# Layer 1's up-projection as seven products of halves, from the third pair of units on

## The chip, the core and the metric

The kernel runs on one core of a Trainium2 chip. The metric is the device time of one execution in microseconds, the median of the runs of one kernel. Five engines of the core work side by side and are ordered by semaphores: TensorE (PE in the profile; PEld are its weight loads), VectorE (DVE), ScalarE (ACT), GpSimd (POOL), and SyncE (SP), on whose queue the loads are issued.

## The reference

Two layers of a backbone work on 512 latent and 256 context tokens of 1024 channels. A layer ends with a gated feed-forward part:

```python
def conv_ffn(xn, w_up, conv_w, w_down):
    u = dwconv(xn @ w_up, conv_w)          # width 3 over positions
    a, gt = jnp.split(u, 2, axis=-1)       # 2 x 2816 columns
    return (a * jax.nn.silu(gt)) @ w_down
```

All is float32. Layer 0 runs it for 768 tokens (latent and context), layer 1, the last one, for the 512 latent tokens only, since the context is no longer needed.

## The kernel before

Activations lie with channels on the 128 partitions and tokens along the free dimension. A float32 product is made of three matmuls of a rounded type (fp32r): each operand is split into a high part, a copy made by ScalarE, and a low part, the difference, made by DVE (`split`, lines 224 and 225). Then high x high, high x low and low x high are summed in PSUM (`mm3`, lines 264 to 266).

The feed-forward part (`ffn`) runs over the 22 blocks of 128 columns of each half of `w_up`, in pairs of two blocks. A pair has two units: g (the gate half) and a (the other half), 256 columns of weights each. Two pairs are a group of four blocks. In program order a group is g, the down-projection of the group before (`down`, held back until here), a, g, a, and then the next group's g. After each unit the convolution follows: one ScalarE step (line 1825) and two DVE steps (lines 1826 and 1828) a block; a g block then gets Silu (line 1834), an a block is multiplied with its g block on POOL (line 1843) and split for the down-projection (lines 1844 and 1845). The down-projection adds its PSUM result to the residual on DVE (line 1872). The last group's down-projection is `gemm_tail`.

A unit is computed in one of two ways:

- `gemm_fm`: for each of the two blocks a load of 128x1024 weights, a split, and 8 x 3 matmuls for each segment of tokens (512 latent, and 256 context in layer 0). The convolution reads PSUM directly.
- `gemm7` (lines 308 to 368): Strassen's method in Winograd's form on a unit seen as two by two halves (channels 0 to 511 and 512 to 1023; its two blocks) times two by two halves of the tokens. POOL makes four sums of halves of the weights (`half`, line 321); four weight tiles are split, w0, w23 and w1 of 128x1024 with the low part on DVE and w4 of 128x512 with the low part on POOL; seven products of 12 matmuls over half of the tokens (`prod`, line 334) use four PSUM tiles, of which three accumulate a second product; two ScalarE copies and five DVE sums (lines 353 to 365) bring the results to the SBUF tiles `c`, which the convolution reads.

The tokens' side of the seven products is made once by `norm_sums` (line 622): sums of halves of the tokens' parts `xh` and `xl` on DVE (line 633 and the two lines in `less`), split into the tiles `T`; the last one, `last_sum`, overwrites a quarter of `xh` and `xl` once the plain units are done. `norm_sums` is called with lowered priority beside the a unit of the second pair, and `x7` is set after it. In the kernel before this happens only where all 768 tokens are worked on (`nt == NT`), that is in layer 0: there pairs three to eleven (18 units) run `gemm7`, in layer 1 all units run `gemm_fm`, and the first g unit `gemm_first`.

Buffers: raw weights have 4 tiles of 128x1024 (tag `wraw`), the split weights 3 high and 3 low tiles (tags `wh`, `wl`), `s23` two and `s4` one; the pool `q6` has 11 tiles, shared by `R` and `T`, the split activations of the down-projection and the tail's weights. The order of each engine's instructions is set ahead by a planner (Tile), from the order of the program, priorities and its own estimates; on the chip each engine runs its list in order.

Of the kernel before, what the change touches and what calls it, by code (L numbers as in the profile page):

```python
# [10 lines left out]
F32R = mybir.dt.float32r  # L11
# [9 lines left out]
NT = SEQ + CTX  # L21
# [84 lines left out]
class Kernel:  # L106
# [515 lines left out]
    def norm_sums(self):  # L622


        nc, N = self.nc, self.N
        nm, n = N["nm"], N["nt"] // 2
        xh, xl = N["x"]
        q = lambda v, k, t: v[:, 4 * k:4 * k + 4, n * t:n * t + n]
        R = [self.q6(f"{nm}R{i}").rearrange("p (k t) -> p k t", k=4) for i in range(2)]
        T = {}  # L630

        def op(o, a, b, op):
            nc.vector.tensor_tensor(out=o, in0=a, in1=b, op=op)

        def diff(i, j, k):

            for o, v in zip(R, (xh, xl)):
                op(o, q(v, *j).bitcast(F32), q(v, *k).bitcast(F32), ALU.subtract)
            op(R[0], R[0], R[1], ALU.add)

        def less(o, j, a):
            op(o, q(xh, *j).bitcast(F32), a, ALU.subtract)
            op(o, o, q(xl, *j).bitcast(F32), ALU.add)

        def split(i, v):
            T[i] = [self.q6(f"{nm}T{p}{i}", F32R).rearrange("p (k t) -> p k t", k=4) for p in "hl"]
            self.split(*T[i], v)
        diff(1, (0, 1), (0, 0))
        split(1, R[0])
        less(R[1], (1, 1), R[0])  # L650
        split(3, R[1])
        less(R[0], (1, 0), R[1])
        split(4, R[0])
        diff(2, (1, 1), (0, 1))
        T[2] = q(xh, 0, 1), q(xl, 0, 1)

        def last():
            self.split(*T[2], R[0])
        return (xh, xl, T), last
# [1147 lines left out]
    def ffn(self, l, xs, nt):  # L1807
        nc = self.nc
        nm = f"f{l}"
        segb = [(0, SEQ)] + ([(SEQ, NT)] if nt == NT else [])  # L1810
        U, U2 = self.I["w_up"][l], self.I["w_down"][l]
        FG = 4
        down = None
        for f0 in range(0, NFF, FG):
            fn = min(FG, NFF - f0)
            gh, gl = [], []
            for p0 in range(0, fn, 2):
                keep = {}

                def conv(ch, res, tag):  # L1820
                    w = [self.V("fv", 132 * l + 44 * k + ch) for k in range(3)]
                    a = self.st(f"{nm}{tag}")
                    for ps, (s, e) in res:
                        n = e - s
                        nc.scalar.activation(a[:, s:e], ps, AF.Copy, scale=w[1])
                        nc.vector.scalar_tensor_tensor(out=a[:, s + 1:e], in0=ps[:, 0:n - 1], scalar=w[0],
                                                       in1=a[:, s + 1:e], op0=ALU.mult, op1=ALU.add)
                        nc.vector.scalar_tensor_tensor(out=a[:, s:e - 1], in0=ps[:, 1:n], scalar=w[2],  # L1828
                                                       in1=a[:, s:e - 1], op0=ALU.mult, op1=ALU.add)
                    return a  # L1830

                def done_g(b, ps):
                    a = conv(NFF + f0 + p0 + b, ps, f"g{f0}{p0}{b}")
                    nc.scalar.activation(a[:, :nt], a[:, :nt], AF.Silu)  # L1834
                    keep[b] = a

                def done_a(b, ps):
                    a = conv(f0 + p0 + b, ps, f"a{f0}{p0}{b}")
                    if b == 0:
                        gh.extend(self.pairs(f"{nm}gh{f0}{p0}", 1, F32R))  # L1840
                        gl.extend(self.pairs(f"{nm}gl{f0}{p0}", 1, F32R))
                    h = gh[-1][:, b, :nt]
                    nc.gpsimd.tensor_tensor(out=a[:, :nt], in0=a[:, :nt], in1=keep[b][:, :nt], op=ALU.mult)  # L1843
                    nc.scalar.copy(h, a[:, :nt])  # L1844
                    nc.vector.tensor_tensor(out=gl[-1][:, b, :nt], in0=a[:, :nt], in1=h.bitcast(F32), op=ALU.subtract)  # L1845

                if f0 + p0 == 0:
                    self.gemm_first(KD, xs, done_g, f"{nm}g{f0}{p0}")
                    x7 = None
                elif x7:  # L1850
                    self.gemm7(U, D_FF + 128 * (f0 + p0), x7, nt, done_g, f"{nm}g{f0}{p0}")
                else:
                    self.gemm_fm(U, D_FF + 128 * (f0 + p0), 256, KD, xs, done_g, f"{nm}g{f0}{p0}")
                if down and f0 + FG < NFF:
                    self.gemm_fm(*down)
                    down = None
                if f0 + p0 == 2 and nt == NT:
                    with self.high(-3000):
                        sums, last_sum = self.norm_sums()
                if x7:  # L1860
                    self.gemm7(U, 128 * (f0 + p0), x7, nt, done_a, f"{nm}a{f0}{p0}")
                else:
                    self.gemm_fm(U, 128 * (f0 + p0), 256, KD, xs, done_a, f"{nm}a{f0}{p0}")
                    if f0 + p0 == 2 and nt == NT:
                        x7 = sums
                        last_sum()
            segs = [((a, b), Blocks(gh, a, b), Blocks(gl, a, b)) for a, b in segb]

            def done_d(j, res):
                hv = self.hview(j)  # L1870
                for ps, (a, b) in res:
                    nc.vector.scalar_tensor_tensor(out=hv[:, a:b], in0=ps,
                                                   scalar=self.ada[l][:, 40 + j, (a >= SEQ):(a >= SEQ) + 1], in1=hv[:, a:b],
                                                   op0=ALU.mult, op1=ALU.add)
            if down:
                self.gemm_fm(*down)
            down = (U2[128 * f0:128 * (f0 + fn), :], 0, D, fn, segs, done_d, f"{nm}d{f0}")
        last = l == DEPTH - 1
        if not last:
            self.norm_begin(l + 1, 0, NT)  # L1880

        def done_t(j, seg, ps):
            done_d(j, [(ps, seg)])
            if not last:
                self.norm_sq(j, *seg, nc.vector if j % 2 else nc.gpsimd)
                if j == 5 and seg[0]:
                    rbs[seg[0] - 256, seg[0]] = self.norm_rs(seg[0] - 256, seg[0])
                if j == KD - 1 and seg[1] == nt:
                    rbs[seg] = self.norm_rs(*seg)
            elif j % 4 == 3:  # L1890
                self.store(j // 4, *seg)
        rbs = {}
        self.gemm_tail(down[0], segs, done_t, f"{nm}t",
                       None if last else (self.I["w_in"][l + 1], C_K, KD, f"c{l + 1}0k"))
        for seg, rb in rbs.items():
            self.norm_fin(*seg, rb)
        return None if last else self.N["xs"]
# [157 lines left out]
```

## Time and profile before

| | us |
|---|---|
| median of 3 runs | 2658.55 (2657.56 to 2661.77) |
| the profiled execution's own time | 2659.69 |
| its span | 2657.9 |
| layer 0's feed-forward part, first seven-product unit to tail | 1078 to 1543 |
| layer 1's feed-forward part, first unit to end | 2274 to 2658 |
| TensorE busy over the span | 2586.3 (97%) |

A page of the profile gives busy times of each engine; windows give them by stretch; a timeline gives single instructions with start and duration, and behind it, in brackets, how long the engine was idle before it and what released it. Matmuls overlap, so the duration of one (0.28 to 0.40 us) is longer than the distance from one start to the next; TensorE's pace is read from starts. Names such as f1a42p read: f, layer 1, a unit, group starting at block 4, pair 2 of it, p for PSUM (c and u for SBUF tiles, w0h and w0l for the high and low part of a weight tile, r for a raw weight tile).

### The profile page before, as it was taken

How to read it: one execution, taken by the hardware profiler on the slowest of the kernel's cores; microseconds unless marked ns; L12 is line 12 of the kernel's file. 1: busy time of each engine (PE TensorE's matmuls, PEld its weight loads, DVE VectorE, ACT ScalarE, POOL GpSimd, SP SyncE). 2: the span in 40 equal slices, each digit the busy share in tenths (PEclk: the TensorE clock that was granted, in tenths of full speed). 3: DMA queues.
4: the chain of work that ended last, by engine and by line, in shares of the span. 5: the costliest groups of instructions: out<-in, count | busy, mean ns of one | idle time of the engine just before them, and what ended most of it. 6: DMA issues, size and time to landing. Idle time of an engine off the chain costs nothing.

```text
span 2657.9 us, 44659 instructions
## 1 busy us (share of the span) xinstructions
PE 2586.3 (97%) x17185; PEld 2235.7 (84%) x17185; DVE 1689.9 (64%) x3599; ACT 1042.6 (39%) x2305; POOL 420.8 (16%) x348
## 2 busy tenths in 40 slices
PE   7999999999999999999999999999999999999999
PEld 5887988788888898899999988888877888888887
DVE  5766566756533648676787777856676646655555
ACT  4433446332422225343343454344633333433332
POOL 1000000000110421264245220000000103100000
PEclk9999999999999999999999999999999999999999
DMA  8354333556747423422212343522367674333332
GB/s 278 100 174 136 98 98 94 145 148 181 217 131 257 145 76 107 131 68 76 80 56 72 96 134 106 158 69 74 113 189 220 193 261 150 88 94 94 95 103 76
DMA packets 485222, 344.19 MB, mean 129 GB/s; under 512 B 48167, under 2 KB 450321, under 8 KB 484241
## 3 DMA queue, kind: packets, MB, share of 16 engines
q1 hardware_dynamic: 484721, 338.19, 42.7%
q8 instruction: 135, 2.21, 0.3%
q10 hardware_dynamic: 288, 3.15, 0.3%
q14 instruction: 78, 0.64, 0.1%
HBM read 285.23 MB, written 56.03 MB: 128 GB/s over the span
## 4 chain that ended last, share of the span: by engine, by line
PE 80%; DVE 8%; DMA 6%; issue 2%; ACT 1%; SPq 1%; POOL 1%; DVEq 0%; ACTq 0%; POOLq 0%
PE mg04p L265 2%; PE mg04p L266 2%; PE mg04p L264 2%; PE adp L541 1%; PE y0p L264 1%; PE y0p L265 1%; PE y0p L266 1%; PE mg14p L264 1%; PE mg14p L266 1%; PE mg14p L265 1%; PE y1p L264 1%; PE y1p L265 1%; PE y1p L266 1%; DMA ad<-ada_w 1%; PE y0op L265 1%
## 5 line engine op out<-in xcount | busy, mean ns | idle before, releaser
L1843 POOL TENSOR_TENSOR f1a<-f1a,f1g 128x512 f32<-128x512 f32 x22 | 28.5, 1295 | 312.1 <-DVE f1a L1828 292.6
L1843 POOL TENSOR_TENSOR f0a<-f0a,f0g 128x768 f32<-128x768 f32 x22 | 52.5, 2389 | 95.6 <-DVE f0a L1828 95.6
L541 PE MATMUL adp<-ad,s 128*32 128x256 f32 x640 | 54.4, 394 | 0.1
L1765 POOL TENSOR_TENSOR y0a<-y0a,y0g 128x768 f32<-128x768 f32 x16 | 33.2, 2078 | 118.1 <-DVE y0g L1762 115.8
L1120 POOL TENSOR_TENSOR m0qz<-m0qz,m0e 64x512 f32<-64x512 f32 x12 | 16.6, 1383 | 166.5 <-DVE b0a3P L1338 69.4
L544 ACT COPY adr<-adp 128x256 f32<-128x256 f32 x40 | 14.8, 371 | 49.4 <-PE adp L541 48.1
L541 PEld LDWEIGHTS adp<-ad,s 128*32 128x32 f32 x640 | 18.5, 110 | 18.5 <-issue 6.9
L1845 DVE TENSOR_TENSOR f0gl<-f0a,f0gh 128x768 fp32r<-128x768 f32 x22 | 28.3, 1287 | 8.9 <-ACT f0gh L1844 8.9
L1765 POOL TENSOR_TENSOR y1a<-y1a,y1g 128x512 f32<-128x512 f32 x16 | 24.2, 1514 | 60.6 <-DVE y1g L1762 60.6
L1844 ACT CAST f0gh<-f0a 128x768 fp32r<-128x768 f32 x22 | 18.4, 838 | 34.9 <-POOL f0a L1843 34.9
L1026 ACT ACTIVATE mg0t<-mg04p 128x512 f32<-128x512 f32 (+1 forms) x40 | 19.4, 486 | 26.2 <-PE mg04p L266 21.7
L1762 DVE SCALAR_TENSOR_TENSOR y0g<-y0g,y0p 128x512 f32<-128x512 f32 (+1 forms) x32 | 17.3, 548 | 15.4 <-PE y0p L266 14.0
L1120 POOL TENSOR_TENSOR m1qz<-m1qz,m1e 64x512 f32<-64x512 f32 x8 | 10.6, 1331 | 102.8 <-DMA m1qz<-aq 32.6
L1109 DVE SCALAR_TENSOR_TENSOR m0mb<-m0mb,g0a,cst 128x128 f32<-128x128 f32 x48 | 16.3, 398 | 16.4 <-DMA m0mb<-g0rd 15.5
L1834 ACT ACTIVATE f1g<-f1g 128x512 f32<-128x512 f32 x22 | 13.9, 630 | 32.5 <-DVE f1g L1828 32.5
L1834 ACT ACTIVATE f0g<-f0g 128x768 f32<-128x768 f32 x22 | 18.5, 846 | 20.5 <-DVE f0g L1828 20.5
L1786 DVE SCALAR_TENSOR_TENSOR hr<-y0op,y0gh,hr 128x512 f32<-128x512 f32 (+1 forms) x16 | 9.9, 616 | 25.5 <-PE y0op L266 25.5
L1182 POOL TENSOR_TENSOR rt<-rc,rw 128x256 f32<-128x256 f32 x4 | 4.2, 1042 | 119.7 <-DVE c00kq L1385 58.5
L1845 DVE TENSOR_TENSOR f1gl<-f1a,f1gh 128x512 fp32r<-128x512 f32 x22 | 15.1, 685 | 10.9 <-ACT f1gh L1844 10.7
L1742 DVE TENSOR_TENSOR y0l<-y0ld,y0h 128x768 fp32r<-128x768 f32 x12 | 12.8, 1090 | 11.6 <-ACT y0h L1741 11.6
L1844 ACT CAST f1gh<-f1a 128x512 fp32r<-128x512 f32 x22 | 13.5, 616 | 16.6 <-POOL f1a L1843 16.6
L1111 ACT ACTIVATE m0mb<-m0mb 128x512 f32<-128x512 f32 x12 | 7.6, 631 | 30.8 <-DVE m0mb L1109 25.3
(4525 smaller groups left out, 10177.4 us busy)
## 6 DMA issues: line engine op xcount, KB each, us to landing
ad<-ada_w SPq DMA_DIRECT2D x96, 512.0 KB, 4.1
mg04r<-w_in SPq DMA_DIRECT2D x20, 512.0 KB, 5.1
mg14r<-w_in SPq DMA_DIRECT2D x20, 512.0 KB, 5.9
y0g<-mg SPq DMA_DIRECT2D x24, 384.0 KB, 4.1
mg<-mg0t SPq DMA_DIRECT2D x24, 256.0 KB, 2.7
y0r<-w_branch SPq DMA_DIRECT2D x12, 512.0 KB, 3.5
mg<-mg1t SPq DMA_DIRECT2D x24, 256.0 KB, 4.2
y1r<-w_branch SPq DMA_DIRECT2D x12, 512.0 KB, 3.8
```

The source lines that it names most:

```text
L264: nc.tensor.matmul(o, hv[:, k, :], xh[:, k, :], start=(k == 0), stop=False)
L265: nc.tensor.matmul(o, hv[:, k, :], xl[:, k, :], start=False, stop=False)
L266: nc.tensor.matmul(o, lv[:, k, :], xh[:, k, :], start=False, stop=(k == nk - 1))
L541: nc.tensor.matmul(ps[32 * j:32 * j + 32, 0:256], self.s32[:, 2 * k:2 * k + 32], raw[:, j, :], start=(q == 0), stop=(q == 1), tile_positio ...
L1026: nc.scalar.activation(s, o, AF.Tanh, scale=0.5)
L1120: nc.gpsimd.tensor_tensor(out=qd[r, d], in0=qd[r, d], in1=e2[r], op=ALU.mult)
L1762: nc.vector.scalar_tensor_tensor(out=(a if i == BR[0] else gt)[:, s:e], in0=gt[:, s:e], scalar=1.0, in1=ps, op0=ALU.add, op1=ALU.mult)
L1765: nc.gpsimd.tensor_tensor(out=a[:, :nt], in0=a[:, :nt], in1=gt[:, :nt], op=ALU.add)
L1834: nc.scalar.activation(a[:, :nt], a[:, :nt], AF.Silu)
L1843: nc.gpsimd.tensor_tensor(out=a[:, :nt], in0=a[:, :nt], in1=keep[b][:, :nt], op=ALU.mult)
L1844: nc.scalar.copy(h, a[:, :nt])
L1845: nc.vector.tensor_tensor(out=gl[-1][:, b, :nt], in0=a[:, :nt], in1=h.bitcast(F32), op=ALU.subtract)
```

## The change

`norm_sums` and `x7` no longer ask for all 768 tokens, so layer 1 too runs its pairs three to eleven (18 units) through `gemm7`, with halves of 256 tokens. The tiles `R` and `T` are cut to the size that the tokens need (4 x 256 columns of 1536). Nothing else differs; the order of units and down-projections in the program is the one that layer 0 has.

```diff
@@ norm_sums
-        R = [self.q6(f"{nm}R{i}").rearrange("p (k t) -> p k t", k=4) for i in range(2)]
+        R = [self.q6(f"{nm}R{i}")[:, :4 * n].rearrange("p (k t) -> p k t", k=4) for i in range(2)]
...
-            T[i] = [self.q6(f"{nm}T{p}{i}", F32R).rearrange("p (k t) -> p k t", k=4) for p in "hl"]
+            T[i] = [self.q6(f"{nm}T{p}{i}", F32R)[:, :4 * n].rearrange("p (k t) -> p k t", k=4) for p in "hl"]
@@ ffn
-                if f0 + p0 == 2 and nt == NT:
+                if f0 + p0 == 2:
                     with self.high(-3000):
                         sums, last_sum = self.norm_sums()
                 if x7:
                     self.gemm7(U, 128 * (f0 + p0), x7, nt, done_a, f"{nm}a{f0}{p0}")
                 else:
                     self.gemm_fm(U, 128 * (f0 + p0), 256, KD, xs, done_a, f"{nm}a{f0}{p0}")
-                    if f0 + p0 == 2 and nt == NT:
+                    if f0 + p0 == 2:
                         x7 = sums
                         last_sum()
```

## Rows read from the trace of the kernel before

**Rows 1.** The page: its span, and each engine's busy time.
```profile
span 2657.9 us, 44659 instructions
...
PE 2586.3 (97%) x17185; PEld 2235.7 (84%) x17185; DVE 1689.9 (64%) x3599; ACT 1042.6 (39%) x2305; POOL 420.8 (16%) x348
```

**Rows 2.** Windows, layer 1: group, its down-projection, the start; length, busy (instructions), clock.
```profile
core 0: us, PE busy (x) PEld busy (x) DVE busy (x) ACT busy (x) POOL busy (x), PEclk, DMA share, GB/s
2337.93:2404.70 66.77, 66.77 (x290) 54.13 (x289) 34.56 (x44) 22.72 (x33) 5.18 (x4) 1.00 0.33 95
2337.93:2359.91 21.98, 21.98 (x98) 18.03 (x97) 12.79 (x17) 6.99 (x11) 0.00 (x0) 1.00 0.49 144
2294.00:2336.00 42.00, 42.00 (x188) 34.12 (x187) 24.78 (x31) 20.13 (x28) 5.18 (x4) 1.00 0.26 75
```

**Rows 3.** Timeline of PE, layer 1 (start, us): first matmuls of consecutive units.
```profile
2382.30 0.40 PE L264 MATMUL f1a42p<-n11xh,f1a42s0h 128*128 128x512 f32 x1
...
2393.49 0.40 PE L264 MATMUL f1g80p<-n11xh,f1g80s0h 128*128 128x512 f32 x1
```

**Rows 4.** Timeline of PE, layer 0's context tokens: first and last of 24 matmuls.
```profile
1064.71 0.28 PE L264 MATMUL f0a02p<-n01xh,f0a02s0h 128*128 128x256 f32 x1
...
1067.42 0.28 PE L266 MATMUL f0a02p<-n01xh,f0a02s0l 128*128 128x256 f32 x1
```

**Rows 5.** Timeline of PE, layer 0: first matmuls of consecutive seven-product units.
```profile
1228.45 0.34 PE L334 MATMUL f0a80x<-n01xh,f0a80w0h 128*128 128x384 f32 x1
...
1243.06 0.34 PE L334 MATMUL f0g82x<-n01xh,f0g82w0h 128*128 128x384 f32 x1
```

**Rows 6.** Windows, layer 0: four seven-product units.
```profile
1135.02:1197.35 62.33, 60.94 (x348) 59.99 (x347) 51.61 (x66) 29.83 (x46) 35.71 (x21) 1.00 0.20 57
```

**Rows 7.** Waits of PE, layer 0's seven-product units: total, times, longest (us).
```profile
PE f0a162x L334 <- POOL f0a162w4l L225: 2.2, 1, 2.2
PE f0a42x L334 <- DVE f0a42c L357: 0.8, 1, 0.8
```

**Rows 8.** The page's costliest groups, layer 1: busy, mean ns | idle before.
```profile
L1843 POOL TENSOR_TENSOR f1a<-f1a,f1g 128x512 f32<-128x512 f32 x22 | 28.5, 1295 | 312.1 <-DVE f1a L1828 292.6
...
L1845 DVE TENSOR_TENSOR f1gl<-f1a,f1gh 128x512 fp32r<-128x512 f32 x22 | 15.1, 685 | 10.9 <-ACT f1gh L1844 10.7
```

**Rows 9.** Instructions of a line or tile: count, min/median/max ns, first and last start.
```profile
L321 POOL TENSOR_TENSOR f0a42s<-f0a42r,f0a42r x2: 1300/1300/1301, 1142.8 to 1146.6; 128x512 f32<-128x512 f32 x2
...
L225 DVE TENSOR_TENSOR f1a00s1l<-f1a00r,f1a00s1h x1: 1212/1212/1212, 2297.3 to 2297.3; 128x1024 fp32r<-128x1024 f32 x1
...
L225 DVE TENSOR_TENSOR f1d8s3l<-f1d8r,f1d8s3h x1: 681/681/681, 2475.1 to 2475.1; 128x512 fp32r<-128x512 f32 x1
...
L1826 DVE SCALAR_TENSOR_TENSOR f1a<-f1a42p,vec,f1a x2: 742/743/744, 2390.1 to 2395.3; 128x511 f32<-128x511 f32 x2
```

**Rows 10.** Timelines of POOL and DVE, layer 0, 1145 to 1151 us.
```profile
1145.37 1.31 POOL L225 TENSOR_TENSOR f0a40w4l<-f0a40s,f0a40w4h 128x512 fp32r<-128x512 f32 x1
1146.64 1.30 POOL L321 TENSOR_TENSOR f0a42s<-f0a42r,f0a42r 128x512 f32<-128x512 f32 x1
1147.89 2.29 POOL L321 TENSOR_TENSOR f0g42s<-f0g42r,f0g42s 128x512 f32<-128x512 f32 x1
...
1146.68 2.33 DVE L225 TENSOR_TENSOR f0g42w0l<-f0g42r,f0g42w0h 128x1024 fp32r<-128x1024 f32 x1 [2.45 <-ACT f0g42w0h L224]
```

**Rows 11.** Timelines of POOL and DVE, layer 0, around 1157 us.
```profile
1156.82 1.29 POOL L321 TENSOR_TENSOR f0g80s<-f0g80r,f0g80r 128x512 f32<-128x512 f32 x1 [6.63 <-DVE f0a L1828]
...
1157.08 1.30 DVE L1828 SCALAR_TENSOR_TENSOR f0a<-f0a40c,vec,f0a 128x255 f32<-128x255 f32 x1
```

**Rows 12.** Timelines of PE and ACT, layer 0: the sixth product, the next unit's w0.
```profile
1145.58 0.34 PE L334 MATMUL f0a40x<-n01Th,f0a40w1h 128*128 128x384 f32 x1
...
1145.60 1.05 ACT L224 CAST f0g42w0h<-f0g42r 128x1024 fp32r<-128x1024 f32 x1 [3.51 <-PE f0a40x L334]
```

## The prediction, made before the changed kernel ran

> **What bounds the kernel now.** I read the page's busy line first: TensorE (PE) is busy 97% of the span, so only fewer TensorE columns, or stalls of TensorE, move the end [rows 1]. Then the stretch that the change touches, by windows. In layer 1's feed-forward part one group is two pairs of units: the down-projection of the group before (21.98 us), then four up-projection units (a, g, a, g). It takes 66.77 us and TensorE is busy for all of it, at a granted clock of 1.00, the 2.4 GHz level; VectorE (DVE) is busy 34.56 us of it and GpSimd (POOL) 5.18 us [rows 2]. So here TensorE alone sets the pace, and the other engines have room. Last I read the stretch of layer 0 that already runs the seven products, because there the same helper shows what it asks of the other engines: there POOL is busy 35.71 of 62.33 us and DVE 51.61 [rows 6].
>
> **What the change takes away.** A unit now is 48 matmuls of 512 columns. From the first of one unit to the first of the next it is 2393.49 - 2382.30 = 11.19 us, 0.233 us each [rows 3]. After the change it is 7 x 4 x 3 = 84 matmuls of 256 columns. The 256-column matmuls of layer 0's context tokens run 23 steps in 2.71 us, 0.118 each [rows 4]; layer 0's 384-column products run 84 in 14.61 us, 0.174 each, or 0.116 scaled to 256 [rows 5]. I take 0.117: 9.83 us a unit, 1.36 us less. There are 18 such units (9 pairs from the third on, a and g), so TensorE loses 24.5 us of work. Four units then need 39.3 us.
>
> A rule weighed here: the Trainium skill, TensorE: Matmul & The Clock Gate, section Back-to-back issue gap, gives N/2.4 + 2.5 ns for a warm matmul, 216 ns at 512 columns and 109 at 256. Both rows are slower than that. By the page (an estimate from its formula) a unit would go from 10.36 to 9.17 us and the loss of work would be 21.4 us and not 24.5; I keep the rows.
>
> **What it adds beside TensorE.** Durations are of undisturbed executions [rows 8, 9, 10]. Per unit POOL gets four sums of halves of 128x512 at 1.30 us and one low part of w4 at 1.31: 6.5 us. DVE splits three weight tiles of 1024 (1.22 us each, 3.65 us) where it split two, and adds five sums of 256 columns that read PSUM. ScalarE gets one more 1024 copy, one of 512 and two small ones; it is busy 22.72 of 66.77 us now [rows 2], so that is no bound. The loads on SP's queue keep their number and size, but both loads of a unit now stand ahead of its splits; four raw buffers cover that, and I cost it at nothing while the split of a unit's second tile frees its buffer a unit ahead. The tail's four weight tiles get their buffers only when the sums are done, under the last 21.98 us down-projection: nothing.
>
> The convolution keeps its four DVE steps (0.743 us each), but their first operand moves from PSUM (names ending in p) to an SBUF tile (c). That matters, because two operations that both read SBUF twice do not run together. A POOL sum starts at 1146.64 and takes 1.30 us; the DVE split that starts at 1146.68 takes 2.33 us in place of 1.22, and ends 1.07 us after the POOL sum does. The next POOL sum starts at 1147.89, takes 2.29, and ends 1.17 us after that split [rows 10]. A convolution step of 255 columns, started under a POOL sum, takes 1.30 us and ends 0.27 us after it [rows 11]. So these operations form **one shared queue**, and behind a waiting one the whole in-order DVE or POOL stands still, the PSUM sums that TensorE waits for included.
>
> The queue per unit, undisturbed: POOL 6.5, splits 3.65, convolution 2.98, together 13.13 us; an a unit adds two products (1.295) and two low parts (0.685), 3.96 us. Four units: 60.4. Some of it can lie under the down-projection: seven sums of halves (9.1) and two splits (2.43) of the first two units, and the last unit's convolution (2.98); the first two down splits (0.68 each, 1.37) come in. That leaves **47.3 us of queue in 39.3 us of TensorE work**. By holds alone, as the overlapped pairs show (1.07 for a split, 1.17 for a POOL operation, 0.53 for 512 columns, twice the 0.27), the same count is 40.2 us; that is the lower end. The upper end: in layer 0 the same count (the 512-column steps scaled by 1.5) is 55.7 us and the stretch took 62.33 [rows 6], 1.12 times as long, although TensorE's need there was 4 x 14.61 = 58.4 us; 1.12 x 47.3 = 52.9 us. The rows are near neither end (layer 0's queue was not the longest of its needs), so I take the middle, 46.5 us: 7.2 us of stall a stretch. Three stretches have four units: 21.7 us. The last has five (no down-projection between its last two): 49.2 us of TensorE work, queue 51.4 to 67.6, middle 59.5, a stall of 10.3.
>
> A rule weighed here: the Trainium skill, SBUF — State Buffer, section Who interferes with whom, says that a DVE instruction with two SBUF inputs contends with a GpSimd one that reads SBUF, and that the loser blocks for the whole instruction. Rows 10 show the blocking, but the hold is some 0.15 us shorter than the instruction. By the page's letter the queue is 47.3 us (60.4 in the last stretch), the stalls 24 + 11 + 2 us, and the time about 2671 us.
>
> **The start.** The sums of the tokens' halves are new in layer 1: ten DVE operations of 1024 columns and four splits, 14 x 1.22 = 17.1 us. From 2294 to 2336 DVE is busy 24.78 of 42.00 us [rows 2], so 17.2 us are free: it just fits while no POOL sum is in the way. Bounds 0 to 6 us (five waits of 1.17); I take 2.
>
> **The sum.** -24.5 + 21.7 + 10.3 + 2 = +9.5 us. The profiled execution took 2659.7 us (span 2657.9), 1.1 above the median, so the median goes to about 2668 us. With every lower end it is -24.5 + 2.7 + 2.2 + 0 = -19.6 us, 2639 us; with every upper end -24.5 + 40.8 + 18.4 + 6 = +40.7 us, 2699 us.
>
> **The rivals.**
> *Faster: the queue compresses.* Where DVE and POOL always have work, each operation's start-up lies under the other's hold, and the stretch needs 40.2 us of queue, hardly over TensorE's 39.3. Then only stalls of layer 0's kind remain: a PSUM sum behind convolution steps (0.8 us), a w4 low part behind a POOL product (2.2 us) [rows 7]; its stretch is 3.9 us over TensorE's need. Three such stretches and one of five (4.9) cost 16.6 us: -7.9 us net, 2651 us; with half of these stalls -16.2 us, 2642; I put this rival at 2647 us. It decides from the point where a stretch needs less than 44 us. For it: layer 0 loses little at a count of 55.7 us in 58.4. Against it: there TensorE was still the longer one.
> *No difference.* A stretch of 44 to 45.5 us: stalls of about 24 us, 2653 to 2664.
> *Much slower: the written order.* The order of each engine's instructions is fixed beforehand, and w0 of the next unit can be split only when the fifth product is done (ScalarE starts it at 1145.60, as the sixth product starts) [rows 12]; two products later it is needed. That window shrinks from 4.2 to 2.8 us, while ScalarE 1.05 + DVE 1.22 + one POOL hold 1.17 make 3.4. At 0.6 us for each of w0 and w23 beside the queue's stalls this gives +9.5 + 18 x 1.2 = +31 us, 2690 us.
> *That it does nothing* can't be: the test on the token count is the only thing that kept layer 1 out.
>
> **How the numbers follow.** A run of this kernel can tell about 0.2%, 5.3 us, from no change. Forecast 2668, its own range 2664 to 2680: 0.38. Much slower, 2680 to 2699: 0.12. No difference: 0.18. Faster: 0.32. The range leaves out the outermost tenth on either side: 2643 to 2691.
>
> **What would show it.** A step right: 256-column products at 0.117 us in layer 1; DVE and POOL both above 75% busy between down-projections; splits and convolution steps at 1.2 to 2.4 us and not 0.74 to 1.22; TensorE idle before products that need w0, w23 or w4, released by DVE or POOL, 6 to 8 us a stretch. Wrong: a group near 61.3 us (21.98 + 39.3) would refute the shared queue as the bound; a 256-column pitch above 0.125 would shift the fault to TensorE; stalls on a load would make it SP's queue.

## The result, and the profile after

The changed kernel takes 2699.38 us (median of 4 runs, 2691.76 to 2700.76), the kernel before 2659.61 us beside it (4 runs): a ratio of 1.0138, 95% interval 1.0122 to 1.0154. By the medians it is 40 us slower, by the ratio 37. The direction was forecast, at 2668 us; the size was not, and the time lies outside the range. The profiled execution took 2700.17 us, its span is 2698.0 us, 40.1 us longer than before [rows 1].

The page of the changed kernel, span and busy times (us, share of the span, instructions):

```profile
span 2698.0 us, 46414 instructions
...
PE 2578.6 (96%) x17833; PEld 2260.9 (84%) x17833; DVE 1809.1 (67%) x3721; ACT 1086.6 (40%) x2381; POOL 582.8 (22%) x438
```

TensorE's busy time fell by only 7.7 us while the span grew by 40.1: it waits, and some of its busy time is slow. DVE gained 119 us, POOL 162 us [rows 1].

Windows of the changed kernel (length, busy time of each engine, granted clock, DMA): the whole stretch from a80's first matmul to a120's; its four units without the down-projection; the second a unit (a82) alone; and two windows of the start, from g40's first matmul on and around it:

```profile
core 0: us, PE busy (x) PEld busy (x) DVE busy (x) ACT busy (x) POOL busy (x), PEclk, DMA share, GB/s
2450.78:2522.30 71.52, 64.74 (x434) 59.76 (x433) 56.49 (x69) 31.92 (x49) 40.62 (x25) 0.95 0.30 89
2450.78:2500.31 49.53, 42.75 (x338) 41.72 (x336) 41.02 (x47) 23.30 (x36) 34.03 (x20) 0.93 0.22 65
2472.68:2490.51 17.83, 12.43 (x87) 12.02 (x85) 15.97 (x15) 7.29 (x11) 11.14 (x7) 0.81 0.15 45
2332.55:2352.00 19.45, 10.11 (x62) 8.50 (x60) 17.08 (x20) 7.09 (x11) 6.57 (x3) 0.78 0.05 14
2313.00:2346.00 33.00, 26.31 (x133) 21.41 (x131) 31.72 (x31) 12.80 (x18) 16.02 (x8) 0.96 0.11 33
```

A group was 66.77 us with TensorE busy throughout [rows 2]. It is now 71.52, though its work has become 5.4 us shorter. Two columns matter: TensorE is busy 42.75 of 49.53 us in the four units, and the granted clock is no longer 1.00.

Waits of PE in layer 1's feed-forward part of the changed kernel (total us, times, longest):

```profile
PE f1a162x L334 <- DVE f1a162c L357: 6.1, 1, 6.1
PE f1a122x L334 <- DVE f1a122c L357: 4.9, 1, 4.9
PE f1a42x L334 <- DVE f1a42c L357: 4.9, 1, 4.9
PE f1a82x L334 <- DVE f1a82c L357: 4.8, 1, 4.8
PE f1g40x L334 <- ACT n11xh L224: 4.1, 1, 4.1
PE f1g42x L334 <- DVE f1g42c L357: 2.4, 1, 2.4
PE f1g40x L334 <- DVE n11Tl L225: 1.7, 1, 1.7
```

In layer 0 the same wait was 0.8 us [rows 7]. Line 357 is the DVE sum that reads the PSUM tile x7; product 6 (line 362) adds to that tile and so can't start before the sum has read it. What keeps line 357 shows in DVE's timeline (start, us; in brackets idle time before):

```profile
2473.53 1.99 DVE L225 TENSOR_TENSOR f1a82w23l<-f1a82s,f1a82w23h 128x1024 fp32r<-128x1024 f32 x1
2475.44 2.31 DVE L225 TENSOR_TENSOR f1a82w1l<-f1a82r,f1a82w1h 128x1024 fp32r<-128x1024 f32 x1
2477.68 1.77 DVE L1845 TENSOR_TENSOR f1gl<-f1a,f1gh 128x512 fp32r<-128x512 f32 x1
2479.38 3.48 DVE L1826 SCALAR_TENSOR_TENSOR f1g<-f1g82c,vec,f1g 128x511 f32<-128x511 f32 x2
2482.78 0.41 DVE L355 TENSOR_TENSOR f1a82u<-f1a82x,f1a82u 128x256 f32<-128x256 f32 x1
2483.11 2.08 DVE L1828 SCALAR_TENSOR_TENSOR f1g<-f1g82c,vec,f1g 128x511 f32<-128x511 f32 x2
2485.11 0.41 DVE L357 TENSOR_TENSOR f1a82c<-f1a82x,f1a82u 128x256 f32<-128x256 f32 x1
```

DVE is never idle here; it works through its list, and the steps take 1.99 and 2.31 us (splits, 1.21 undisturbed), 1.77 (low part, 0.68) and 1.74 (each of the two L1826 steps, 0.74) [rows 8, 9]. Meanwhile POOL works without a pause:

```profile
2474.40 2.27 POOL L321 TENSOR_TENSOR f1a82s<-f1a82r,f1a82s 128x512 f32<-128x512 f32 x1
2476.64 2.27 POOL L321 TENSOR_TENSOR f1g120r<-f1g120r 128x512 f32<-128x512 f32 x1
2478.99 1.62 POOL L321 TENSOR_TENSOR f1g120s<-f1g120r,f1g120r 128x512 f32<-128x512 f32 x1
2480.57 1.73 POOL L225 TENSOR_TENSOR f1a82w4l<-f1a82s,f1a82w4h 128x512 fp32r<-128x512 f32 x1
2482.38 1.59 POOL L321 TENSOR_TENSOR f1g120s<-f1g120r,f1g120s 128x512 f32<-128x512 f32 x1
```

A sum of halves took 1.30 us alone in layer 0 [rows 9]; here 1.59 to 2.27. On TensorE the wait ends so (duration, and idle time before):

```profile
2485.58 0.58 PE L334 MATMUL f1a82x<-n11Th,f1a82w1h 128*128 128x256 f32 x1 [4.79 <-DVE f1a82c L357]
```

**Where the 40.1 us went**, by starts of the same unit in both traces. Up to the start of g40, 5.8 us: the order of the instructions of DVE, ScalarE and POOL is the same there until the a unit of the second pair, and most of the loss arises near 1460 us, in layer 0. From a162's first matmul to g200's 60th it takes 28.40 us in before, 32.25 in the changed kernel and 28.14 in e1_own_t2, which has the change too. At that place TensorE waits for a low part of w4 on POOL [rows 7]; the last section shows how this wait differs from one execution to the next. So this part is no work of the change; the rest of the 5.8 us I take for the spread from run to run (in the kernels below, the start of g40 lies between 2.3 us earlier and 5.3 us later than in before), which is argued and not shown. From g40 to a40 (the start), 46.59 us in place of 33.18: +13.4. Three stretches, 71.64, 71.52 and 71.50 in place of 66.76 each: +14.4. From a160 to the end: +6.5.

### The profile page after: what moved, and what is told of

Same layout as the page of the kernel before. It is cut to its first block, busy times and chain, and to the rows that moved or that the text cites. A ratio compares the mean times of both kernels' runs of the same rounds, so it can differ in the third digit from the quotient of the medians.

```text
span 2698.0 us, 46414 instructions
## 1 busy us (share of the span) xinstructions
PE 2578.6 (96%) x17833; PEld 2260.9 (84%) x17833; DVE 1809.1 (67%) x3721; ACT 1086.6 (40%) x2381; POOL 582.8 (22%) x438
## 4 chain that ended last, share of the span: by engine, by line
PE 74%; DVE 12%; DMA 6%; issue 3%; ACT 2%; SPq 1%; POOL 1%; DVEq 0%; ACTq 0%; POOLq 0%
PE mg04p L265 2%; PE mg04p L264 2%; PE mg04p L266 1%; PE y0p L264 1%; PE y0p L265 1%; PE adp L541 1%; PE y0p L266 1%; PE mg14p L264 1%; PE mg14p L266 1%; PE mg14p L265 1%; PE y1p L264 1%; PE y1p L265 1%; PE y1p L266 1%; DMA ad<-ada_w 1%; PE y0op L264 1%
## 5 line engine op out<-in xcount | busy, mean ns | idle before, releaser
L1843 POOL TENSOR_TENSOR f1a<-f1a,f1g 128x512 f32<-128x512 f32 x22 | 36.3, 1659 | 53.1 <-DVE f1a L1828 29.5
L541 PEld LDWEIGHTS adp<-ad,s 128*32 128x32 f32 x640 | 18.4, 109 | 19.4 <-issue 6.8
L544 ACT COPY adr<-adp 128x256 f32<-128x256 f32 x40 | 14.8, 369 | 45.6 <-PE adp L541 44.3
L1844 ACT CAST f0gh<-f0a 128x768 fp32r<-128x768 f32 x22 | 18.4, 837 | 34.1 <-POOL f0a L1843 34.1
L1845 DVE TENSOR_TENSOR f1gl<-f1a,f1gh 128x512 fp32r<-128x512 f32 x22 | 26.0, 1184 | 1.3 <-ACT f1gh L1844 1.2
L1742 DVE TENSOR_TENSOR y0l<-y0ld,y0h 128x768 fp32r<-128x768 f32 x12 | 12.8, 1091 | 11.7 <-ACT y0h L1741 11.7
```

The source lines that it names most:

```text
L541: nc.tensor.matmul(ps[32 * j:32 * j + 32, 0:256], self.s32[:, 2 * k:2 * k + 32], raw[:, j, :], start=(q == 0), stop=(q == 1), tile_positio ...
```

## The experiments

All start from the changed kernel. Theory **Q** is the prediction's: the path that DVE and POOL share holds both up. Rival **D**: DVE's own list is too long, whatever POOL does. Later rivals: POOL's list is too long, so that the weights' sums come late; the fallen clock is a cost of its own; the place of a unit in the order counts, not the sum of work. One measure runs through all of them, the stretch from a80 to a120, with DVE's and POOL's busy time in it (the windows of each kernel). The times in the last column are medians of 11, 10 and 5 executions for e3_three, e3_no_g0 and e3_spread, and of a single one for the other experiments; those are compared by their stretches:

| kernel | stretch, us | DVE | POOL | time, us (before beside it) |
|---|---|---|---|---|
| before [rows 2] | 66.77 | 34.56 | 5.18 | 2659.61 |
| changed | 71.52 | 56.49 | 40.62 | 2699.38 (2659.61) |
| e1_half_dve | 70.05 | 59.64 | 12.27 | 2690.37 (2661.69) |
| e1_no_half | 64.25 | 49.07 | 11.65 | 2663.81 (2661.69) |
| e1_own_t2 | 71.51 | 56.39 | 41.11 | 2697.42 (2661.69) |
| e1_late | 71.73 | 56.59 | 41.16 | 2679.41 (2661.69) |
| e2_memset | 64.23 | 49.05 | 20.68 | 2662.52 (2662.59) |
| e3_memset3 | 64.24 | 49.08 | 35.63 | 2659.88 (2662.43) |
| e2_fill | 69.65 | 56.69 | 42.13 | 2687.16 (2662.59) |
| e2_p0, 9 units | 65.81 | 43.88 | 20.89 | 2657.38 (2662.59) |
| e2_three, 13 units | 65.69 | 49.11 | 31.59 | 2656.14 (2662.59) |
| e3_three, the same | 65.68 | 49.54 | 31.35 | 2659.94 (2662.43) |
| e3_no_g0, 13 units | 68.84 | 51.12 | 33.61 | 2666.29 (2662.43) |
| e3_spread, 9 units | 64.17 | 42.67 | 21.17 | 2650.38 (2662.43) |

### Is it the shared path, or DVE's list?

**e1_no_half** leaves out the sums of halves in layer 1 and uses the raw weights in their place.

```diff
         if nt == NT:
             half(s23[:, hi], r0[:, lo], r1[:, lo], ALU.subtract)
             ...
+        else:
+            s23, s4 = r1, r0[:, hi]
```

> In layer 1 the four POOL sums of halves are left out (the products take the raw halves; the result of layer 1's up-projection is another). DVE, ScalarE and TensorE do what they do in the changed kernel. Theory Q: the shared queue of a stretch falls to about 35.6 us, below TensorE's 39.3; a group takes 62 to 64 us and the kernel about 2660 to 2668. Theory D: DVE's list is as long as before, so a group stays at 70 us or more and the kernel at 2692 or more.

The stretch falls to 64.25 us, 7.3 less than in the changed kernel, and DVE, whose own instructions are the same, is busy 49.07 us and not 56.49: 7.4 us less. So the sums on POOL cost the stretch 7.3 of the 10.2 us by which it exceeds its work (21.98 + 39.3 = 61.3 us), and they do it by stretching DVE's steps:

```profile
2438.38:2502.63 64.25, 62.80 (x433) 57.83 (x432) 49.07 (x68) 31.81 (x49) 11.65 (x8) 1.00 0.34 99
```

The other 2.9 us stay without any sum on POOL: 1.45 of them are idle time, in short waits, nearly all for DVE's list.

**e1_half_dve** moves those sums to DVE.

```diff
-                nc.gpsimd.tensor_tensor(out=out, in0=a, in1=b, op=op)
+                (nc.gpsimd if nt == NT else nc.vector).tensor_tensor(out=out, in0=a, in1=b, op=op)
```

> The four sums of halves of each weight tile pair in layer 1 move from POOL to DVE; the result is the same. Theory Q (DVE and POOL operations that read SBUF twice form one shared queue): a sum holds the shared path 0.53 us on DVE against 1.17 on POOL, so the queue of a four-unit stretch falls from 47.3 to about 41.7 us and hardly any operation waits for the other engine; a group goes from 71.5 us in the changed kernel to 63 to 66, the kernel to about 2670 to 2680. Theory D (DVE's own list is too long, POOL is no part of it): DVE gets 16 x 0.68 = 10.9 us more in a group, so a group goes to 75 to 82 us and the kernel above 2715.

70.05 us fits neither theory: hardly anything is shared now, but DVE is busy 59.64 us (49.07 without the sums, and 16 sums of about 0.68), and products wait for its list all the same. The list now also stands still until a unit's weights have landed, 2.75 us ahead of the sums of a82. (The planner also placed TensorE's units otherwise here.) Both theories hold a part: the sharing is what makes DVE's list too long, and there is no room on DVE for the sums themselves.

### Is it what POOL reads, or how long POOL is busy?

**e2_memset** writes the tiles of the sums on POOL by a memset, which reads nothing; **e3_memset3** writes each three times, so that POOL has as much to do as with the sums. Both leave out the sums of halves in layer 1. The diff is that of three; one has no loop.

```diff
-                nc.gpsimd.tensor_tensor(out=out, in0=a, in1=b, op=op)
+                if nt == NT:
+                    nc.gpsimd.tensor_tensor(out=out, in0=a, in1=b, op=op)
+                else:
+                    for _ in range(3):
+                        nc.gpsimd.memset(out, 0.0)
```

> In layer 1 the four POOL sums of halves are replaced by POOL memsets of the same tiles, which read nothing from SBUF (the up-projection of layer 1 is then not computed). POOL's list, its order and who waits for it stay. If the two engines shut each other out while both read SBUF, DVE's splits and convolution steps fall back to 1.22 and 0.74 us while a memset runs, and a group takes 64 to 66 us as in the run without sums. If it is POOL's in-order list and its place between the loads and the splits, a group stays at 69 us or more.

> Leaves out the sums of halves in layer 1: GpSimd writes each tile three times by memset in their place, so that its list is as long as with the sums (3 x 0.525 = 1.58 us for each, against 1.3 us alone and 1.7 to 2.3 us beside VectorE), but reads nothing. If what costs is that GpSimd's sums hold the path to the memory from VectorE, the a80 to a120 stretch stays at the 64 to 65 us that one memset gave. If it is that GpSimd has so much to do that the weights' sums come late, it goes most of the way back to 71.5 us, 68 us or more.

Windows of the kernel with three memsets, the stretch from a80 to a120:

```profile
2434.56:2498.80 64.24, 62.75 (x434) 57.85 (x433) 49.08 (x68) 31.78 (x48) 35.63 (x57) 1.00 0.34 99
```

Against that of the kernel with one memset:

```profile
2437.12:2501.35 64.23, 62.65 (x433) 57.75 (x432) 49.05 (x68) 31.77 (x48) 20.68 (x25) 1.00 0.34 99
```

POOL is busy 15 us longer, and neither the stretch nor DVE moves by more than 0.03 us. POOL's list is not the bound, and its time alone costs nothing. What costs is that POOL's sums read the memory that DVE reads. (A memset also waits for no weights, so it can run earlier than a sum; that alone would not change how long DVE's own steps take, and it is these that differ.)

The Trainium skill, SBUF — State Buffer, section Who interferes with whom, says that a DVE instruction with two SBUF inputs contends with a GpSimd instruction that reads SBUF, and not with one that only writes it. This trace agrees with both halves: 56.49 us of DVE beside sums, 49.05 and 49.08 beside memsets, 49.07 with neither.

### The start

**e1_own_t2** gives the last token sum columns of its own, so that it overwrites nothing that a plain unit still reads.

```diff
+        if N["nt"] < NT:
+            T[2] = [v[:, 0:4, SEQ:NT] for v in (xh, xl)]
```

> The last sum of the tokens' halves goes to columns of the token tiles that layer 1 leaves unused, so that it no longer waits for the plain units to be done with the quarter it overwrote. If the first unit's stall (14.9 us at its place) comes from this wait, its 4.1 us behind ScalarE's copy and 1.2 behind DVE's low part go, and some of the low clock with them: 5 to 8 us faster than the changed kernel, about 2692. If it comes from the 17 us of sums on a DVE that has no room for them, at most 2 us. The groups behind it stay at 71.5 us in both.

From g40 to a40 it takes 46.47 us against 46.59: the wait to overwrite is not the cause.

**e1_late** sets `x7` two units later, after a40; 16 units have seven products.

```diff
-                    if f0 + p0 == 2:
+                    if f0 + p0 == (2 if nt == NT else 4):
                         x7 = sums
```

> Layer 1 takes the seven products from the fourth pair on in place of the third (16 units); the sums of the tokens are made at the same place, with a whole group's time (66.8 us) until they are needed. If the start is a matter of too little DVE time in 42 us, its stall of 14.9 us falls to 3 or less, and the first stretch has two seven-product units only; two units' gain of 1.36 us each is lost: about 2680 to 2686. If the sums are late wherever they stand (a fixed order), the stall moves to the fourth pair and the time stays within 4 us of 2699.

The stall at the start is gone: g40 to a40 takes 33.18 us as before, and no product waits for a token sum. The stretches stay as long as they were, 71.73 us. So the start's loss was that the token sums had too little time on DVE, and it is separate from the stretches' loss. How much of it is POOL's doing, e1_no_half shows: without weight sums on POOL the first token sums take 1.22 us each, and g40 to a40 still takes 42.10 us. Of the 13.4 us, 4.5 go with POOL's sums and 8.9 stay.

```profile
2313.55 1.22 DVE L637 TENSOR_TENSOR n11R<-n11xh 128x1024 f32<-128x1024 f32 x1
```

### The clock

**e2_fill** puts 32 idle 256-column matmuls on a PSUM tile that nothing reads ahead of product 6 of the second a unit of each group. They fill the wait; the work of DVE and POOL stays the same.

```diff
+        if nt < NT and nm[:3] == "f1a" and nm[-1] == "2":
+            fl = self.pa(f"{nm}fl")[:, 0:n]
+            for k in range(32):
+                nc.tensor.matmul(fl, w1[0][:, k % 4, :], xh[:, 0, t0], start=True, stop=True)
         prod(x7, w1, 4, *oft(4), False, True)
```

> The changed kernel, with 32 idle matmuls of 256 columns (3.7 us, to a PSUM tile that nobody reads) put ahead of the sixth product of the a units of second pairs, where TensorE sits idle for 4.8 us and its granted clock then is 0.81 over the unit. If the fallen clock is a cost of its own, these units take 2 to 3 us less each (four of them), and the kernel is 8 to 11 us faster than the changed one. If the clock costs nothing, or the wait for DVE just moves, a group stays at 71.5 us or gets longer by what the fill takes.

Windows of this kernel, the units g82 and a82:

```profile
2454.02:2467.69 13.67, 11.35 (x86) 11.14 (x85) 12.92 (x13) 6.35 (x9) 11.88 (x7) 0.90 0.27 77
2467.69:2481.55 13.86, 13.86 (x117) 13.86 (x117) 12.72 (x13) 6.99 (x11) 8.74 (x6) 0.98 0.13 39
```

a82 takes 13.86 us from start to start and not 17.83, at a granted clock of 0.98 and not 0.81. Part of the wait has moved: g82 ahead of it takes 13.67 us and not 12.01, so the stretch is 1.9 us shorter and not 4.0. From a40's first matmul to the tail's first (f1tp) it takes 288.58 us against 296.85, 8.3 us less; the rest of the difference lies ahead of a40. DVE is busy 56.69 us in the stretch and POOL 42.13, about as in the changed kernel. The planner moved other instructions too, so the 8.3 us (2.1 for each of the four filled units) are not surely the clock's alone; what the clock costs, the changed kernel itself shows, in windows around its wait (the wait, the rest of the unit, the next unit):

```profile
2480.60:2485.58 4.98, 0.20 (x3) 0.01 (x1) 4.92 (x6) 0.93 (x2) 3.30 (x3) 0.76 0.00 0
2485.58:2490.51 4.93, 4.93 (x25) 4.93 (x25) 3.13 (x4) 2.58 (x4) 0.00 (x0) 0.55 0.19 55
2490.51:2500.31 9.80, 9.80 (x87) 9.80 (x85) 7.42 (x13) 5.36 (x10) 4.28 (x3) 1.00 0.10 30
```

After 4.79 us without work TensorE got a granted clock of 0.55, almost the lower of its two levels (1.2 GHz), for the last products of the unit; then 1.00. A unit without a stall takes 9.89 us, this one 17.83: 5.4 us idle; 2.1 us because the 24 matmuls behind the wait took 4.93 us in place of 2.82 (0.1176 each); and 0.4 us at the beginnings and ends of its two waits.

### Fewer units by seven products

If the path is too full, two units of four should leave room. Two tests say which units call `gemm7`; all these kernels have the columns of e1_own_t2. In e3_spread:

```diff
-                elif x7:
+                elif x7 and (nt == NT or (p0 == 2 and f0 > 3)):
...
-                if x7:
+                if x7 and (nt == NT or p0 == 0):
```

The four choices:

| kernel | g units, by pair | a units, by pair |
|---|---|---|
| e2_p0 | first of a group | first of a group |
| e2_three, e3_three | both | first of a group |
| e3_no_g0 | second of a group | both |
| e3_spread | second of a group | first of a group |

The g unit of a group's first pair is the one ahead of the down-projection. g40 stays plain in all of them; a40 is the first unit with seven products.

> Layer 1 takes the seven products only in the units that stand beside a down-projection (a of a group's first pair and g of the next group's first pair, from a40 on: 9 units); the other units stay plain, and the last sum of the tokens gets a place of its own so that the tokens stay whole. Theory Q (the shared DVE and POOL queue overflows only in the middle of four such units in a row): no stall over 1 us in any unit, nothing at the start (over 45 us for the sums), 9 x 1.36 = 12.2 us less than the kernel before: about 2648 to 2651. Rival (each seven-product unit of 256-column halves brings a stall of its own, 1.4 us or more): no faster than the kernel before.

> As the run with 9 units, and the g unit of each group's second pair too (13 units; the a unit of the second pair stays plain). Theory Q: the g unit waits 1 to 2 us for a DVE sum behind the convolution as in the changed kernel (1.4 us idle), so the four more units (5.4 us) are about given back: 2645 to 2653. If what stalled was the a unit of the second pair alone, all 17.7 us are gained: about 2643.

> Nine of layer 1's units by seven products: the first a unit of every four, the g unit right behind it, and the last a unit (one seven-product unit, then another, then two plain ones). If the loss is the sum of elementwise work in a group (theory: the path that VectorE and GpSimd share, with VectorE's list behind it), two units in four leave it room whatever their place, no product waits, and the stretch from one a80 start to a120 start is 66.77 - 2 x 1.36 = 64.05 us; the whole is 9 x 1.36 = 12.2 us below the kernel before. If the seven products cost each time something that the sum of work does not hold, it comes out as the nine units beside the down-projections did: 65.8 us a stretch, some 5 us below the kernel before.

> Thirteen of layer 1's units by seven products (all but the second a unit of every four), the same kernel as the earlier one look, now timed in rounds. By the earlier look 6.5 us below the kernel before, 2653 us, interval within 0.2%; the two stretches' stalls are 1.9 us each before the fourth unit. If the earlier look was helped by the few us by which unchanged stretches vary from run to run, it falls to within 0.2% of before.

> Thirteen units by seven products as in the kernel with all but the second a unit, but it is now the fourth unit of a group (the one ahead of the down-projection) that stays with three, and the second a unit has seven. If the loss follows the sum of elementwise work, the stretch from a80 to a120 is the same as with the other thirteen, 65 to 66.5 us. If it follows what stands where in the order (the second a unit's product 6 behind the first pair's convolutions), the stall of 4.8 us before that product is back: 68 to 69 us a stretch, over 2665 us in all.

**e3_spread** has no wait inside the groups. Its stretch, and the one wait that is left behind a40:

```profile
2428.53:2492.70 64.17, 64.17 (x361) 55.72 (x360) 42.67 (x56) 27.14 (x41) 21.17 (x15) 1.00 0.34 99
```

```profile
PE f1a200x L334 <- DVE f1a200c L357: 0.5, 1, 0.5
```

TensorE is busy all of 64.17 us; 66.77 - 2 x 1.36 = 64.05 was expected. The kernel's median is 2650.38 us, a ratio of 0.9950 to before (95% interval 0.9935 to 0.9964). That is 12 us below the kernel before, where nine units are worth 12.2.

**e2_p0** has as many such units, but the second one stands ahead of the down-projection: 65.81 us, 1.8 over the count, and 2657.38 us in all, above the 2648 to 2651 expected. 0.86 us of it is idle time in three waits (for w1, for the down-projection's first split, for line 357). Another 0.8 us is lost at the same three places: matmuls overlap, so the last one ahead of a wait runs out its whole duration (0.28 us at 256 columns, 0.12 apart in a stream), and the second one behind the wait starts 0.22 us after the first. Each of these waits cost some 0.27 us more than its idle time as the profile counts it.

**e3_three** is 0.9989 of before (0.9980 to 0.9998), a gain of a tenth of a per cent; the single execution of e2_three, the same kernel, had been 6.5 us below before, and short of the 2645 to 2653 us expected for it. **e3_no_g0**, also with thirteen units, is slower than before: 1.0016 (1.0006 to 1.0026). So with as many units and much the same work (DVE 49.54 and 51.12 us, POOL 31.35 and 33.61), the stretch is 65.68 us in one order and 68.84 in the other. The sum of work does not decide this; the place does, as the second half of the expectation had it. POOL's timeline shows why. In e3_no_g0, while g82 is computed, POOL makes the sums for a82:

```profile
2434.49 1.29 POOL L321 TENSOR_TENSOR f1a82s<-f1a82r,f1a82r 128x512 f32<-128x512 f32 x1 [0.25 <-DMA f1a82r<-w_up]
...
2437.99 2.26 POOL L321 TENSOR_TENSOR f1a82r<-f1a82r 128x512 f32<-128x512 f32 x1
2440.33 2.16 POOL L321 TENSOR_TENSOR f1a82s<-f1a82r,f1a82r 128x512 f32<-128x512 f32 x1
```

and DVE's splits of g82 take 1.90 to 1.98 us:

```profile
2434.96 1.90 DVE L225 TENSOR_TENSOR f1g82w0l<-f1g82r,f1g82w0h 128x1024 fp32r<-128x1024 f32 x1 [1.71 <-ACT f1g82w0h L224]
...
2439.36 1.98 DVE L225 TENSOR_TENSOR f1g82w1l<-f1g82r,f1g82w1h 128x1024 fp32r<-128x1024 f32 x1
...
2446.33 0.41 DVE L357 TENSOR_TENSOR f1g82c<-f1g82x,f1g82u 128x256 f32<-128x256 f32 x1
```

In e3_three a82 is plain and needs no sums; the same splits run free:

```profile
2437.00 1.23 DVE L225 TENSOR_TENSOR f1g82w0l<-f1g82r,f1g82w0h 128x1024 fp32r<-128x1024 f32 x1 [1.72 <-ACT f1g82w0h L224]
...
2439.94 1.22 DVE L225 TENSOR_TENSOR f1g82w1l<-f1g82r,f1g82w1h 128x1024 fp32r<-128x1024 f32 x1
...
2444.05 0.42 DVE L357 TENSOR_TENSOR f1g82c<-f1g82x,f1g82u 128x256 f32<-128x256 f32 x1
```

From the first of these to line 357 it is 7.1 us there and 11.4 us in e3_no_g0, where product 6 waits 2.5 us for it. I read this so: down-projection and first unit leave room for two units' sums; each further unit's sums fall into a seven-product unit, whose 9.83 us of TensorE work give DVE too little time, unless a plain unit stands there. Four orders bear this out (the changed kernel's, e3_no_g0's, e3_three's and e3_spread's); as a rule for others it is not tested.

## Why the prediction was right or wrong

**TensorE's work: right.** The changed kernel starts a80 at 2450.78 and g82 at 2460.67 (first matmuls):

```profile
2450.78 0.28 PE L334 MATMUL f1a80x<-n11xh,f1a80w0h 128*128 128x256 f32 x1
...
2460.67 0.28 PE L334 MATMUL f1g82x<-n11xh,f1g82w0h 128*128 128x256 f32 x1
```

9.89 us for 84 matmuls is 0.118 each, 0.117 was taken. e3_spread confirms the worth of a unit.

**The shared queue: right in kind and in the size of its idle time.** Two of the signs named came: splits and convolution steps at 1.74 to 2.3 us, and TensorE idle 6.8 us in a stretch (5.40 in a82, 1.38 in g82), inside the 6 to 8 named, 7.2 forecast. In the three stretches it is idle 8.0, 6.8 and 6.7 us by windows, 21.5 together, 21.7 forecast. The closeness is luck in part: 46.5 us was the middle of 40.2 and 52.9, taken without a row for it, and the count said nothing of where in the order the waits would lie. Two signs did not come. POOL is busy 34.03 of 49.53 us between the down-projections, 69% and not above 75 (DVE 83%). And the wait is not where I looked for it, at w0, w23 or w4 (w23 is late by 0.6 us in a82), but at line 357. The prediction did say that the PSUM sums stand behind a held-up list; the sign that it named was another. Nor is the shared path all: by its count (35.6 us of queue in 39.3) a stretch without POOL's sums has no stall, and e1_no_half still lay 2.9 us over its work, with short waits for DVE's own list.

**The price of a stretch: the step that failed is that a stall was counted as idle time only.** A stretch of four units takes 49.53 us against 39.3 of work, 10.2 us over, not 7.2. Of that 6.8 is idle, 2.1 the slow matmuls behind the long wait, and 1.3 the rest, nearly all at the beginnings and ends of five waits, as in e2_p0. Three stretches cost 30.7 us and not 21.7 (their growth, 14.4, and the 16.3 us of work that twelve units lose), the last one 13.3 and not 10.3 (6.5 + 6.8). No term of the sum held the slow matmuls or the restart behind a stall. In the range's upper end these costs had room (40.8 and 18.4); the range was then cut to 2691. That every upper end together gives 2699 us, the time measured, is chance: the stretches stayed below their ends and the start came to more than twice its own.

**The start: the largest error.** Two us were taken, 0 to 6 the bounds; it cost 14.8 us (13.4, and the 1.36 that g40 was to gain). The step that failed: DVE's free time was counted from 2294, 17.2 us up to 2336, as if the token sums could use all of it. In the changed kernel the first token sum starts only at 2314.06, the first two take 2.31 us each beside POOL, and the last low part is made at 2347.43:

```profile
2314.06 2.31 DVE L633 TENSOR_TENSOR n11R<-n11xh 128x1024 f32<-128x1024 f32 x1
2316.30 2.31 DVE L633 TENSOR_TENSOR n11R<-n11xl 128x1024 f32<-128x1024 f32 x1
...
2341.95 1.66 DVE L633 TENSOR_TENSOR n11R<-n11xh 128x1024 f32<-128x1024 f32 x1
...
2347.43 1.21 DVE L225 TENSOR_TENSOR n11xl<-n11R,n11xh 128x1024 fp32r<-128x1024 f32 x1
```

From 2313 to 2346 DVE is busy 31.72 of 33.00 us, and g40, which starts at 2332.55, gets its last token sum after 2346 (4.1 us of wait for n11xh, 4.7 for others). Free time on an engine ahead of the place where its list puts the work is no cover. The prediction's own condition, no POOL sum in the way, would not have saved it: 8.9 of the 13.4 us stay in e1_no_half. With TensorE idle so often the granted clock was 0.78 over these 19.45 us.

**The rivals.** *Faster* and *no difference* fell: no stretch's four units came under 49.5 us. *Much slower* came near in time (2690) but not in kind: w0 and w23 are not what is late. The written order does decide, as e3_no_g0 and e3_three show, by which sums on POOL lie beside which unit.

**The miss, added up.** By spans the change was forecast at +9.5 us and came to +40.1. The 30.6 us between are 12.8 for the start, 9.0 for three stretches, 3.0 for the last, and the 5.8 us ahead of the changed code.

A rule weighed afresh: the Trainium skill, SBUF — State Buffer, section Summary: rules for kernel authors, says that where DVE has two SBUF inputs while the GpSimd operation reads SBUF, the second to issue is blocked until the first has finished. By that letter the prediction had 24 us of stall for the three stretches, by its own middle 21.7. Their idle time is 21.5 us and their whole loss 30.7; as the middle rested on no row, these runs don't tell one hold from the other.

## What to carry to other kernels

Moving work off the bounding engine pays only while the engines that prepare it keep up, so count for each single unit what lies beside it, not for a whole stretch, and give the cheaper form to as many units as leave none waiting (here nine of eighteen gave 12 us, all eighteen cost 40). Count elementwise work on DVE and POOL as one list where both read SBUF, and count preparation time from where it stands in the engine's list, not from where the engine has gaps. To a stall of TensorE add the restart behind it and the slow matmuls that can follow it (here after 4.79 us, and after about 2 us in half of the executions).

## What the runs showed of the hardware that was not expected

- Sums on POOL that read SBUF made DVE busy 56.49 us for work that takes it 49.07 us without them; memsets on POOL, up to 35.63 us of a 64.24 us stretch, made it no longer (49.08).
- After 4.79 us idle TensorE's granted clock was 0.55 over the next 4.93 us. With the 2.5 us wait in g82 of e3_no_g0 it was 0.90 over that unit, and with the two waits of e3_three before a down-projection (1.2 and 0.5 us) 1.00 over the stretch:

```profile
2436.63:2451.04 14.41, 11.83 (x86) 11.33 (x85) 13.48 (x15) 6.97 (x10) 12.71 (x7) 0.90 0.25 73
```

```profile
2428.81:2494.49 65.68, 63.67 (x397) 56.72 (x396) 49.54 (x63) 29.80 (x45) 31.35 (x20) 1.00 0.33 97
```

- What a wait of about 2 us does to the clock differs from one execution to the next. All these kernels have the same layer 0, and in its unit a162 TensorE waits for POOL [rows 7]. In twelve of the fourteen profiled executions the wait was 1.75 to 2.25 us: in six of these, the kernel before among them, the next 24 matmuls (384 columns) ran at a granted clock of 1.00 and took 4.3 us, in the other six at 0.71 and took 5.8 to 5.9. In the other two, the changed kernel and e1_no_half, the wait was 3.29 us and the clock 0.57 and 0.72. Windows behind this wait in before (2.15 us), e1_late (2.22) and the changed kernel (3.29):

```profile
1459.76:1464.10 4.34, 4.34 (x25) 4.34 (x25) 2.91 (x3) 2.41 (x4) 3.44 (x2) 1.00 0.01 4
1458.59:1464.46 5.87, 5.87 (x25) 5.87 (x25) 3.41 (x5) 2.90 (x5) 3.40 (x2) 0.71 0.16 47
1463.49:1470.49 7.00, 7.00 (x24) 7.00 (x25) 3.15 (x5) 3.23 (x6) 2.42 (x2) 0.57 0.16 45
```

- Unchanged code ahead of the change took up to 8 us longer in one kernel's profiled execution than in another's (the start of g40 lies 2.3 us earlier to 5.8 us later than before). So a single execution says little of a change worth some 5 us: the kernel with thirteen units was 6.5 us below before in one, and 2.5 us by medians.
